# Two down projections by seven streamed products, with the sums of their operands made in gate and up

## The chip, the cores and the metric

The kernel runs on one core of a Trainium2 chip. The metric is the device time of one execution in microseconds (us); less is better. A tile has 128 partitions. Engines: PE (matrix products, into eight banks of PSUM of 128 x 512 f32), PEld (its loading of the stationary operand), DVE, ACT, POOL (elementwise work), SP (issues nearly all DMAs, in order).

## The reference

One decoder layer on x of 1024 tokens x 1024, in float32. Its two feed-forward blocks (FFN1, FFN2) are alike; the mixer between them is not touched by the change.

```python
def swiglu(x, w_gate, w_up, w_down):
    return (jax.nn.silu(x @ w_gate) * (x @ w_up)) @ w_down

x = x + 0.5 * swiglu(rmsnorm(x, ffn1_norm), ffn1_w_gate, ffn1_w_up, ffn1_w_down)
x = x + hybrid_mixer(rmsnorm(x, mix_norm), ...)
x = x + 0.5 * swiglu(rmsnorm(x, ffn2_norm), ffn2_w_gate, ffn2_w_up, ffn2_w_down)
return rmsnorm(x, final_norm)
```

w_gate and w_up are 1024 x 2816, w_down is 2816 x 1024: 22 blocks of 128 hidden features, taken in 11 pairs.

## The kernel before

**Precision.** Every operand of a large product is split in two float32r parts: a high part H (ACT casts it) and a low part L = operand - H (DVE subtracts). A product of blocks is three matmuls per 128 features: H with H, H with L, L with H. `load_w2` loads 128 x 1024 values into a `wraw` (or `xs`) buffer, casts at L204 and subtracts at L205. Loaded weights land in a pool of pairs (wH, wL). FFN1 has four raw buffers and five pairs (`wp` two and three, `wp1` two and two); FFN2's gate and up stage has four raw buffers and four pairs, its down stage four and six.

**Gate and up.** `hidden_tiles` goes over the 11 pairs, for each the gate half and then the up half. Tokens and features are both cut in two, and the four blocks of a half's result come from seven products of sums of blocks instead of eight plain ones. `seven_weights` loads two blocks of 128 weight columns and lets POOL make four sums into a tile wS (L346), of which there is one buffer; casts and subtractions follow (L354, L355). `seven_products` runs the seven products (12 matmuls of 128 x 512 each, L365) in the order 1, 2, 6, 5, 7, 4, 3; ACT copies a bank out (`ev`, L393) and DVE adds a second one to it (L397), giving four tiles `sg` or `su`. The first product of the first two pairs (EARLY = 2) is made before the rest, so these have five products left. ACT applies silu to the gate tiles. Then POOL multiplies su by sg in place (`gate_up`, L423), and SP writes the result to a DRAM buffer `hd[j]` of pair j.

**Down.** `down` runs plain products over chunks of 6, 6, 6 and 4 blocks. For each chunk, the hidden blocks come back from `hd` and the weights from w_down, both through `load_w2`; for each column half and each of eight token tiles, a bank collects all matmuls of the chunk (L537) and DVE adds half of it to x (L539). The x tiles are loaded in the first chunk, one ahead of each token tile (L552). The last chunk goes token tile by token tile, both halves, and calls `done(t)`, which in FFN1 writes x, normalises it and turns it for the mixer, and in FFN2 normalises it and writes the output. In FFN1 `done` also loads the mixer's first two weights (`first`).

**Order.** All instructions are put in order at compile time, engine by engine, by a scheduler that walks a model of the machine and takes the ready instruction of best priority (program order); each engine and each queue then runs its own list strictly in order, and waits on semaphores. A buffer of a tile tag with n buffers is given out again when all users of the earlier tile are done.

Of the kernel before, what the change touches and what calls it, by code (L numbers as in the profile page):

```python
# [9 lines left out]
F32 = mybir.dt.float32  # L10
# [6 lines left out]
P = 128  # L17
# [46 lines left out]
class Weights:  # L64
# [25 lines left out]
def psum(C, tag):  # L90
    return C.pp.tile([P, 512], F32, name=tag, tag=tag, bufs=BANKS[tag])
# [329 lines left out]
def gate_up(C, out, sg, hd, i, a, eng=None):  # L421

    (eng or C.nc.gpsimd).tensor_tensor(out=out, in0=out, in1=sg, op=ALU.mult)  # L423
    C.nc.sync.dma_start(hd[:, i, a * 512:a * 512 + 512], out)


EARLY = 2
# [54 lines left out]
    return banks  # L482


def hidden_tiles(C, XB, wg, wu, hd, banks, whole):

    nc = C.nc

    def tiles(tag, bufs):
        return [[C.fp.tile([P, 512], F32, name=tag, tag=tag, bufs=bufs) for _ in range(2)] for _ in range(2)]  # L490

    for j in range(DFF // P // 2):
        rest = ((1, 1), (1, 0), (0, 1)) if j < EARLY else ((0, 0), (1, 1), (1, 0), (0, 1))

        def half(w, tag, bufs):
            early = banks.pop(0) if j < EARLY else None
            out = tiles(tag, bufs) if whole else None
            W = seven_weights(C, w, j * 256, early is not None)
            out = out or tiles(tag, bufs)
            first = j == 0 and w is wg and not whole  # L500
            seven_products(C, W, XB, out, early, PIECES if first else WHOLE, "tC" if first else "tA")
            return out

        g = half(wg, "sg", 5)
# [7 lines left out]
def down(C, tc, x, src, wd, hd, chunks, last, done, side):  # L512

    nc = C.nc

    def hidden(f0, n, a):
        tiles = []
        for j in range(f0 // 2, (f0 + n) // 2):
            to = [C.fp.tile([P, SLOT], F32R, name=t, tag=t, bufs=8 if not C.last else 4) for t in ("hidH", "hidL")]
            H, L = load_w2(C, hd[j][:, :, a * 512:a * 512 + 512], 2, 512, to)  # L520
            tiles += [(H[:, i], L[:, i]) for i in range(2)]
        return tiles

    def wtiles(f0, n, nh):
        W = []
        for k2 in range(0, n, 2):
            r = (f0 + k2) * P
            H, L = load_w2(C, wd[r:r + 256, nh * 512:nh * 512 + 512].rearrange("(k p) n -> p k n", p=P), 2, 512)
            W += [(H[:, 0], L[:, 0]), (H[:, 1], L[:, 1])]
        return W  # L530

    def one(t, nh, hid, W):
        ps = psum(C, "tC" if nh else "mm")
        m = slice(t % 4 * P, t % 4 * P + P)
        seq = [(hid[t // 4][k][i], W[k][w]) for k in range(len(W)) for i, w in ((0, 0), (0, 1), (1, 0))]
        for i, (h, w) in enumerate(seq):
            nc.tensor.matmul(ps, h[:, m], w, start=i == 0, stop=i == len(seq) - 1)  # L537
        xs = x[t][:, nh * 512:nh * 512 + 512]
        nc.vector.scalar_tensor_tensor(xs, ps, 0.5, xs, op0=ALU.mult, op1=ALU.add)  # L539

    f0 = 0
    C.last = False
    with tc.tile_pool(name="hid", bufs=1, side=side, reuse_waits="tile") as C.fp:
        for n in chunks:
            hid = []
            for nh in (0, 1):
                W = wtiles(f0, n, nh)
                for t in range(NT):
                    if nh == 0 and t % 4 == 0:
                        hid.append(hidden(f0, n, t // 4))  # L550
                    if f0 == nh == 0:
                        nc.sync.dma_start(x[t], src[t * P:t * P + P])  # L552
                    one(t, nh, hid, W)
            f0 += n
    C.last = True
    with tc.tile_pool(name="hidl", bufs=1, side=side, reuse_waits="tile") as C.fp:
        last()
        Ws = [wtiles(f0, 4, 0), wtiles(f0, 4, 1)]
        hid = [hidden(f0, 4, a) for a in (0, 1)]
        for t in range(NT):  # L560
            for nh in (0, 1):
                one(t, nh, hid, Ws[nh])
            done(t)

# [935 lines left out]
def ffn2(C, tc, I, out, hs):  # L1500

    nc = C.nc
    wg, wu = I["ffn2_w_gate"], I["ffn2_w_up"]
    C.XB = {}
    for i, names in enumerate((("B11", "B21"), ("T2", "T1"))):
        for q, n in enumerate(names):
            C.XB[n] = [b[i][:, q * 4:q * 4 + 4, :] for b in (C.hH, C.hL)]
    with ExitStack() as st:
        x2p = st.enter_context(tc.tile_pool(name="x2", bufs=1, side="right"))

        x2 = dict((t, x2p.tile([P, D], F32, name=f"x2{t}")) for t in (0, 4, 1, 5, 2, 6, 3, 7))
        late, W2 = merge_out(C, tc, I, x2)
        with tc.tile_pool(name="xb2", bufs=1, reuse_waits="tile") as xb:
            for n in ("T3", "B22", "T4"):
                C.XB[n] = [xb.tile([P, 4, 512], F32R, name=n + h) for h in "HL"]
            with tc.tile_pool(name="lo", bufs=1) as lo:
                banks = early_products(C, I, late, W2, lo)
            st.close()
            with tc.tile_pool(name="f2", bufs=1, reuse_waits="tile") as C.fp:
                C.wp.add(C.tp, 2, 0, "xs")  # L1520
                hidden_tiles(C, C.XB, wg, wu, C.hd, banks, True)
    hs.close()
    with tc.tile_pool(name="x3", bufs=1, reuse_waits="tile") as xp:
        C.wp.add(xp, 0, 2)
        x = [xp.tile([P, D], F32, name=f"x{t}") for t in range(NT)]

        def done(t):
            y = xp.tile([P, D], F32, name="y", tag="xg", bufs=3)
            nc.gpsimd.tensor_tensor(out=y, in0=x[t], in1=C.gF, op=ALU.mult)  # L1529
            r = rstd(C, x[t], xp)  # L1530
            nc.scalar.activation(y[:, :512], y[:, :512], AF.Copy, scale=r)  # L1531
            nc.sync.dma_start(out[t * P:t * P + P, :512], y[:, :512])
            nc.vector.tensor_scalar(y[:, 512:], y[:, 512:], r, None, op0=ALU.mult)  # L1533
            nc.sync.dma_start(out[t * P:t * P + P, 512:], y[:, 512:])

        def last():
            C.gF = load_gain(C, I["final_norm"])

        down(C, tc, x, C.x2d, I["ffn2_w_down"], C.hd, (6, 6, 6), last, done, "right")


def layer(tc, I, out):
# [4 lines left out]
    with ExitStack() as st, ExitStack() as hs:  # L1547
# [17 lines left out]
        C.hd = [C.dp.tile([P, 2, T], F32, name=f"hd{j}") for j in range(DFF // P // 2)]  # L1565
        C.hH, C.hL = [None, None], [None, None]

        def open_h(a):
# [12 lines left out]
def ffn1(C, tc, I, open_h):  # L1581

    nc = C.nc
    with ExitStack() as st:
        C.wp.add(st.enter_context(tc.tile_pool(name="wp1", bufs=1)), 2, 2)
        C.tp = st.enter_context(tc.tile_pool(name="tp1", bufs=1))
        consts(C, I)
        with tc.tile_pool(name="xb", bufs=1) as xb:
            XB = {n: [xb.tile([P, 4, 512], F32R, name=n + h) for h in "HL"] for n in XBLOCKS if n != "T4"}
            wg, wu = I["ffn1_w_gate"], I["ffn1_w_up"]  # L1590
            with tc.tile_pool(name="s1", bufs=1) as sp:
                banks = early_tiles(C, tc, XB, I, wg, wu, C.hd, sp)
            with tc.tile_pool(name="f1", bufs=1, reuse_waits="tile") as C.fp:
                hidden_tiles(C, XB, wg, wu, C.hd, banks, False)
# [4 lines left out]
        with tc.tile_pool(name="x1", bufs=1, reuse_waits="tile") as xp:  # L1599
            x = []  # L1600
            for t in range(NT):
                x.append(xp.tile([P, D], F32, name=f"x{t}"))
# [12 lines left out]
                if t > 1:  # L1615
                    late.pop(0)()

            down(C, tc, x, I["x"], I["ffn1_w_down"], C.hd, (6, 6, 6), lambda: open_h(1), done1, "left")

            C.begun = {}  # L1620
            for c0, (H, L), at in ((C_QA, W[0], None), (C_KA, W[1], {5: late[1]})):
# [30 lines left out]
```

## Time and profile before

| | |
|---|---|
| Median of three runs | 2651.56 us (2649.98, 2651.56, 2662.56) |
| Profiled execution, own time | 2658.93 us |
| its span, first to last instruction | 2657.2 us |
| mean granted TensorE clock | 0.99 |
| FFN1's down matmuls (L537) | from 470.1 to 724.4 us |
| FFN2's down matmuls (L537) | from 2397.2 to 2643 us |

In the profile, "PE L537 MATMUL mm<-wH,hidH 128*128 128x512 f32 x1" is a matmul of line 537 into a bank named mm, with stationary 128 x 128 and moving 128 x 512; the first number is its start, the second its length, as far as matmuls are recorded singly. The end of a matmul is modelled, so its pace is read from starts. "[1.98 <-PE tC L365]" is the idle time of the engine just before an instruction, and what ended it. Rows of groups give busy us, the mean in ns, then idle time before and its releasers. SPq rows are DMAs at the time SP issues them; a length there that covers several DMAs includes SP's waiting between them.

### The profile page before, as it was taken

What the parts mean: (1) busy time and instruction counts of PE and PEld (TensorE: products, weight loads), DVE (VectorE), ACT (ScalarE), POOL (GpSimd) and SP (SyncE); (2) the same over time, 40 slices, a digit from 0 to 9 for tenths busy, and PEclk for the clock granted to TensorE, in tenths of its full rate; (3) what the DMA queues carried; (4) which work ended last, traced back from release to release, by engine and by line L of the source; (5) the groups of instructions that cost most, each with busy time, mean ns of one, the idle gap of its engine ahead of it and who ended that gap; (6) DMA issues with size and microseconds to landing.
All of it is one profiled execution on the core that took longest, in us unless ns stands there. A gap on an engine that the chain in (4) does not pass through costs nothing. (4 is left out here: it accounts for less than half of the span.)

```text
span 2657.2 us, 34573 instructions
## 1 busy us (share of the span) xinstructions
PE 2574.7 (97%) x13007; PEld 2140.1 (81%) x13007; DVE 1459.2 (55%) x3276; ACT 1017.2 (38%) x1706; POOL 469.6 (18%) x378
## 2 busy tenths in 40 slices
PE   6999999999999999999999999999999999999997
PEld 5888888788788888887887888877877888887886
DVE  6444444432744447868877877445764444444326
ACT  5333333211434338445444543343433333332113
POOL 5534452000200000000000000000004445430002
PEclk9999999999999999999999999999999999999999
DMA  5322223522331232223312122366533223226211
GB/s 152 91 87 88 83 73 98 202 95 64 113 95 52 75 78 58 60 73 94 83 54 63 55 62 76 122 217 227 183 99 115 76 84 88 84 80 222 99 56 72
DMA packets 298807, 262.10 MB, mean 99 GB/s; under 512 B 39856, under 2 KB 232592, under 8 KB 298640
## 3 DMA queue, kind: packets, MB, share of 16 engines
q1 hardware_dynamic: 298640, 259.90, 32.0%
q8 instruction: 102, 1.67, 0.3%
q14 instruction: 65, 0.53, 0.1%
HBM read 195.26 MB, written 58.29 MB: 95 GB/s over the span
## 5 line engine op out<-in xcount | busy, mean ns | idle before, releaser
L229 PE MATMUL mm<-hH,wH 128*128 128x512 f32 x1072 | 438.4, 409 | 0.0
L229 PE MATMUL mm<-hH,wL 128*128 128x512 f32 x1072 | 419.6, 391 | 0.1
L229 PE MATMUL mm<-hL,wH 128*128 128x512 f32 x1072 | 418.4, 390 | 0.0
L204 ACT CAST wH<-wraw 128x1024 fp32r<-128x1024 f32 (+1 forms) x138 | 143.8, 1046 | 293.6 <-PE mm L537 124.3
L205 DVE TENSOR_TENSOR wL<-wraw,wH 128x1024 fp32r<-128x1024 f32 (+1 forms) x138 | 169.5, 1230 | 127.0 <-ACT wH L204 122.2
L229 PEld LDWEIGHTS mm<-hH,wL 128*128 128x128 f32 x1072 | 201.4, 188 | 45.5 <-DVE wL L205 0.5
L229 PEld LDWEIGHTS mm<-hH,wH 128*128 128x128 f32 x1072 | 202.2, 189 | 40.4 <-issue 3.6
L229 PEld LDWEIGHTS mm<-hL,wH 128*128 128x128 f32 x1072 | 202.4, 189 | 36.0
L355 DVE TENSOR_TENSOR wL<-wS,wH 128x1024 fp32r<-128x1024 f32 x88 | 126.8, 1442 | 161.7 <-ACT wH L354 160.9
L346 POOL TENSOR_TENSOR wS<-wraw 128x512 f32<-128x512 f32 x66 | 84.1, 1296 | 564.0 <-PE tA L296 323.6
L423 POOL TENSOR_TENSOR su<-su,sg 128x512 f32<-128x512 f32 x84 | 133.2, 1596 | 185.6 <-DVE su L397 161.5
L354 ACT CAST wH<-wS 128x1024 fp32r<-128x1024 f32 x88 | 92.5, 1053 | 152.0 <-PE tC L365 110.3
L393 ACT COPY ev<-mm 128x512 f32<-128x512 f32 (+1 forms) x118 | 68.4, 580 | 199.8 <-PE mm L365 199.8
L537 PE MATMUL mm<-wH,hidH 128*128 128x512 f32 x352 | 138.2, 393 | 2.8 <-DVE x L539 2.0
L537 PE MATMUL mm<-wH,hidL 128*128 128x512 f32 x352 | 137.7, 391 | 2.6 <-DVE hidL L205 2.6
L537 PE MATMUL mm<-wL,hidH 128*128 128x512 f32 x352 | 137.5, 390 | 1.3 <-DVE wL L205 1.3
L537 PE MATMUL tC<-wH,hidH 128*128 128x512 f32 x352 | 137.2, 390 | 1.5 <-ACT wH L204 1.5
L537 PE MATMUL tC<-wL,hidH 128*128 128x512 f32 x352 | 137.8, 392 | 0.5 <-DVE wL L205 0.5
L537 PE MATMUL tC<-wH,hidL 128*128 128x512 f32 x352 | 137.7, 391 | 0.0
L922 POOL MEMSET xp<- 128x3 f32 x24 | 2.4, 100 | 584.4 <-DVE ka L728 244.6
L539 DVE SCALAR_TENSOR_TENSOR x<-mm,x 128x512 f32<-128x512 f32 x64 | 43.9, 688 | 105.6 <-PE mm L537 104.5
L539 DVE SCALAR_TENSOR_TENSOR x<-tC,x 128x512 f32<-128x512 f32 x64 | 44.0, 688 | 88.2 <-PE tC L537 88.2
(432 smaller groups left out, 5997.4 us busy)
## 6 DMA issues: line engine op xcount, KB each, us to landing
wraw<-in_w_in_dram SPq DMA_DIRECT2D x64, 512.0 KB, 4.0
wraw<-in_ffn_w_gate_dram SPq DMA_DIRECT2D x48, 512.0 KB, 4.6
hd<-su SPq DMA_DIRECT2D x84, 256.0 KB, 3.2
wraw<-in_ffn_w_down_dram SPq DMA_DIRECT2D x33, 512.0 KB, 4.6
wraw<-hd SPq DMA_DIRECT2D x33, 512.0 KB, 4.6
wraw<-in_ffn_w_up_dram SPq DMA_DIRECT2D x26, 512.0 KB, 5.0
xs<-in_ffn_w_up_dram SPq DMA_DIRECT2D x22, 512.0 KB, 3.9
wraw<-in_w_branch_b_dram SPq DMA_DIRECT2D x16, 512.0 KB, 4.3
```

The lines of the kernel that those rows point to most:

```text
L204: nc.scalar.copy(H[:, :width], raw[:, :width])
L205: (nc.gpsimd if C.pool_split else nc.vector).tensor_tensor(out=L[:, :width], in0=raw[:, :width], in1=H[:, :width].bitcast(F32), op=ALU.sub ...
L229: ins = nc.tensor.matmul(ps, w[:, k, :], x[:, k, :], start=k == 0 and i == 0, stop=k == kt - 1 and i == 2)
L346: nc.gpsimd.tensor_tensor(out=out, in0=p, in1=q, op=op)
L354: nc.scalar.copy(H[:, :n], srcs)
L355: eng.tensor_tensor(out=L[:, :n], in0=srcs, in1=H[:, :n].bitcast(F32), op=ALU.subtract)
L393: nc.scalar.copy(v[:, s], ps[:, s])
L423: (eng or C.nc.gpsimd).tensor_tensor(out=out, in0=out, in1=sg, op=ALU.mult)
L537: nc.tensor.matmul(ps, h[:, m], w, start=i == 0, stop=i == len(seq) - 1)
L539: nc.vector.scalar_tensor_tensor(xs, ps, 0.5, xs, op0=ALU.mult, op1=ALU.add)
L922: nc.gpsimd.memset(xp[:, 0:3], 0.0)
```

## The change

1. In `hidden_tiles`, from the third pair on (j >= EARLY), the result is no longer written to `hd`. `hidden_blocks` makes four sums of the pair's four blocks on POOL, over the gate tiles and one up tile, and writes seven blocks (A11, A12, A22, S1 to S4) to DRAM, in chunks of two pairs (nine pairs: four chunks of two and one of one).
2. In the up half of the next pair, behind its weight sums, `down_blocks` loads two blocks of rows of w_down, makes four sums of their halves on POOL (one of them into an up tile of the earlier pair) and writes them to DRAM (T1 to T4). The last pair's come after the loop.
3. `down` runs the nine pairs as seven products, in the order of `DOWN`. A product goes chunk by chunk: a load of its hidden operand, a load of its weight operand, and for four token tiles six matmuls per tile into four banks that stay open over the product. Two sets of four banks alternate, and some products add to what their set already holds. After each product DVE adds half of four banks to x. The x tiles are loaded behind the fourth and fifth slot of the first product and in the third.
4. Pairs 0 and 1 stay plain and come last, token tile by token tile, with `done(t)` as before.
5. Pools: the hidden tiles have four buffers instead of eight and are laid out ahead of x; FFN1's `wp1` has one pair instead of two (four in all); FFN2's down stage gets two raw buffers more (six in all, six pairs); the gain for the last norm is loaded ahead of the down stage, into the buffer that `down_blocks` uses; tiles for results of FFN2's gate and up are taken behind the weights from the second pair on.

```diff
 def gate_up(C, out, sg, hd, i, a, eng=None):
     (eng or C.nc.gpsimd).tensor_tensor(out=out, in0=out, in1=sg, op=ALU.mult)
-    C.nc.sync.dma_start(hd[:, i, a * 512:a * 512 + 512], out)
+    if hd is not None:
+        C.nc.sync.dma_start(hd[:, i, a * 512:a * 512 + 512], out)
...
+def hidden_blocks(C, u, g, n):
+    (a11, a21), (a12, a22) = u
+    s1, s2, s3, s4 = g[1][1], g[0][0], a21, g[1][0]
+    for out, p, q, op in ((s1, a21, a22, ALU.add), (s3, a11, a21, ALU.subtract), (s2, s1, a11, ALU.subtract), (s4, a12, s2, ALU.subtract)):
+        C.nc.gpsimd.tensor_tensor(out=out, in0=p, in1=q, op=op)
+    c, i = slot(n)
+    for name, v in (("A11", a11), ("A12", a12), ("A22", a22), ("S1", s1), ("S3", s3), ("S2", s2), ("S4", s4)):
+        C.nc.sync.dma_start(C.ab[name][c][:, i, :], v)
+
+def down_blocks(C, wd, n, t3):
+    nc = C.nc
+    X, Y = [pool.tile([P, SLOT], F32, name=tag, tag=tag, bufs=1) for pool, tag in ((C.tp, "gB"), (C.fp, "wY"))]
+    for i, r in enumerate((X, Y)):
+        nc.sync.dma_start(r, wd[(2 * n + i) * P:(2 * n + i + 1) * P])
+    lo, hi = slice(0, 512), slice(512, 1024)
+    for out, p, q in ((t3, Y[:, hi], X[:, hi]), (X[:, hi], X[:, hi], X[:, lo]), (Y[:, hi], Y[:, hi], X[:, hi]), (Y[:, lo], Y[:, lo], Y[:, hi])):
+        nc.gpsimd.tensor_tensor(out=out, in0=p, in1=q, op=ALU.subtract)
+    c, i = slot(n)
+    for name, v in (("T3", t3), ("T1", X[:, hi]), ("T2", Y[:, hi]), ("T4", Y[:, lo])):
+        nc.sync.dma_start(C.tb[name][c][:, i, :], v)
...
         def half(w, tag, bufs):
             early = banks.pop(0) if j < EARLY else None
-            out = tiles(tag, bufs) if whole else None
+            out = tiles(tag, bufs) if whole and j == 0 else None
             W = seven_weights(C, w, j * 256, early is not None)
+            if w is wu and due:
+                down_blocks(C, wd, *due.pop())
             out = out or tiles(tag, bufs)
...
         for i, a in rest:
-            gate_up(C, u[i][a], g[i][a], hd[j], i, a)
+            gate_up(C, u[i][a], g[i][a], hd[j] if j < EARLY else None, i, a)
+        if j >= EARLY:
+            hidden_blocks(C, u, g, j)
+            due.append((j, u[0][0]))
+    down_blocks(C, wd, *due.pop())
+
+DOWN = (("A11", "B11", 0, True, (0, 0)), ("A12", "B21", 1, True, (0, 0)), ("S2", "T2", 0, False, (0, 1)), ("S1", "T1", 1, True, (1, 1)),
+        ("S3", "T3", 0, False, (1, 1)), ("S4", "B22", 1, False, (0, 1)), ("A22", "T4", 0, False, (1, 0)))
+
+def down(C, x, src, wd, hd, done):
...
+    def hidden(v, n):
+        return load_w2(C, v, n, 512, [C.fp.tile([P, SLOT], F32R, name=t, tag=t, bufs=4) for t in ("hidH", "hidL")])
...
+    def mms(ps, m, hid, W, n, first, stop, more=False):
+        seq = [(hid[i][:, k], W[w][:, k]) for k in range(n) for i, w in ((0, 0), (0, 1), (1, 0))]
+        for i, (h, w) in enumerate(seq):
+            nc.tensor.matmul(ps, h[:, m], w, start=first and i == 0, stop=stop and i == len(seq) - 1, skip_group_check=more)
+
+    banks = [[psum(C, tag) for tag in tags for _ in range(2)] for tags in (("mm", "tM"), ("tA", "tC"))]
+    for a, b, z, begin, (half, nh) in DOWN:
+        for c, v in enumerate(C.ab[a]):
+            n = v.shape[1]
+            A, B = hidden(v, n), weights(b, c, n)
+            for t in range(4):
+                mms(banks[z][t], slice(t * P, t * P + P), A, B, n, begin and c == 0, c == len(C.ab[a]) - 1, not begin)
+            for t in {("B11", 3): (0, 1), ("B11", 4): (2, 3)}.get((b, c), (4 + c,) if b == "T2" and c < 4 else ()):
+                nc.sync.dma_start(x[t], src[t * P:t * P + P])
+        for t in range(4):
+            add(half * 4 + t, nh, banks[z][t])
+    Ws = [[weights_plain(C, wd, c, nh) for c in range(EARLY)] for nh in (0, 1)]
+    hid = [[hidden(hd[c][:, :, q * 512:q * 512 + 512], 2) for c in range(EARLY)] for q in (0, 1)]
+    for t in range(NT):
+        for nh in (0, 1):
+            ps = psum(C, "mm" if nh else "tC")
+            for c in range(EARLY):
+                mms(ps, slice(t % 4 * P, t % 4 * P + P), hid[t // 4][c], Ws[nh][c], 2, c == 0, c == EARLY - 1)
+            add(t, nh, ps)
+        done(t)
...
 (ffn2)
-    with tc.tile_pool(name="x3", bufs=1, reuse_waits="tile") as xp:
-        C.wp.add(xp, 0, 2)
+    with tc.tile_pool(name="hid", bufs=1, side="right", reuse_waits="tile") as C.fp, tc.tile_pool(name="x3", bufs=1, reuse_waits="tile") as xp:
+        C.wp.add(xp, 2, 2)
...
 (ffn1)
-        C.wp.add(st.enter_context(tc.tile_pool(name="wp1", bufs=1)), 2, 2)
+        C.wp.add(st.enter_context(tc.tile_pool(name="wp1", bufs=1)), 2, 1)
```

More of the change, by code (lines that the diff above doesn't have):

```diff
@@ L482, in early_tiles, with slot, hidden_tiles @@
     return banks
-def hidden_tiles(C, XB, wg, wu, hd, banks, whole):
+def slot(n):
+    n -= EARLY
+    return n // 2, n % 2
+def hidden_blocks(C, u, g, n):
[17 more added lines that the diff above has]
+        nc.sync.dma_start(C.tb[name][c][:, i, :], v)
+def hidden_tiles(C, XB, wg, wu, wd, hd, banks, whole):
     nc = C.nc
@@ L490, in tiles @@
         return [[C.fp.tile([P, 512], F32, name=tag, tag=tag, bufs=bufs) for _ in range(2)] for _ in range(2)]
+    due = []
     for j in range(DFF // P // 2):
@@ L508, in hidden_tiles @@
         for i, a in rest:
-            gate_up(C, u[i][a], g[i][a], hd[j], i, a)
-def down(C, tc, x, src, wd, hd, chunks, last, done, side):
-    nc = C.nc
[L516 to L537, printed above, removed]
+            gate_up(C, u[i][a], g[i][a], hd[j] if j < EARLY else None, i, a)
@@ new lines, in hidden_tiles, with weights, add @@
+        if j >= EARLY:
[5 more added lines that the diff above has]
+def down(C, x, src, wd, hd, done):
+    nc = C.nc
+    def hidden(v, n):
+        return load_w2(C, v, n, 512, [C.fp.tile([P, SLOT], F32R, name=t, tag=t, bufs=4) for t in ("hidH", "hidL")])
+    def weights(name, c, n):
+        if name in C.tb:
+            v = C.tb[name][c]
+        else:
+            i, q = int(name[1]) - 1, int(name[2]) - 1
+            j = EARLY + 2 * c
+            v = wd.rearrange("(j i p) n -> i p j n", i=2, p=P)[i][:, j:j + n, q * 512:q * 512 + 512]
+        return load_w2(C, v, n, 512)
+    def add(t, nh, ps):
@@ L538, in one @@
         xs = x[t][:, nh * 512:nh * 512 + 512]
         nc.vector.scalar_tensor_tensor(xs, ps, 0.5, xs, op0=ALU.mult, op1=ALU.add)
[L541 to L563, printed above, removed]
+    def mms(ps, m, hid, W, n, first, stop, more=False):
+        seq = [(hid[i][:, k], W[w][:, k]) for k in range(n) for i, w in ((0, 0), (0, 1), (1, 0))]
+        for i, (h, w) in enumerate(seq):
+            nc.tensor.matmul(ps, h[:, m], w, start=first and i == 0, stop=stop and i == len(seq) - 1, skip_group_check=more)
@@ new lines, in down, with weights_plain @@
+    Ws = [[weights_plain(C, wd, c, nh) for c in range(EARLY)] for nh in (0, 1)]
[7 more added lines that the diff above has]
+        done(t)
+def weights_plain(C, wd, c, nh):
+    return load_w2(C, wd[c * 256:c * 256 + 256, nh * 512:nh * 512 + 512].rearrange("(k p) n -> p k n", p=P), 2, 512)
@@ L1520, in ffn2 @@
                 C.wp.add(C.tp, 2, 0, "xs")
-                hidden_tiles(C, C.XB, wg, wu, C.hd, banks, True)
+                hidden_tiles(C, C.XB, wg, wu, I["ffn2_w_down"], C.hd, banks, True)
     hs.close()
-    with tc.tile_pool(name="x3", bufs=1, reuse_waits="tile") as xp:
-        C.wp.add(xp, 0, 2)
+    with tc.tile_pool(name="hid", bufs=1, side="right", reuse_waits="tile") as C.fp, tc.tile_pool(name="x3", bufs=1, reuse_waits="tile") as xp:
+        C.wp.add(xp, 2, 2)
         x = [xp.tile([P, D], F32, name=f"x{t}") for t in range(NT)]
@@ L1534, in done @@
             nc.sync.dma_start(out[t * P:t * P + P, 512:], y[:, 512:])
-        def last():
-            C.gF = load_gain(C, I["final_norm"])
-        down(C, tc, x, C.x2d, I["ffn2_w_down"], C.hd, (6, 6, 6), last, done, "right")
+        C.gF = load_gain(C, I["final_norm"])
+        down(C, x, C.x2d, I["ffn2_w_down"], C.hd, done)
 def layer(tc, I, out):
@@ L1564, in layer @@
         C.ud = [C.dp.tile([32, 1024], F32, name=f"ud{f}") for f in range(2)]
-        C.hd = [C.dp.tile([P, 2, T], F32, name=f"hd{j}") for j in range(DFF // P // 2)]
+        C.hd = [C.dp.tile([P, 2, T], F32, name=f"hd{j}") for j in range(EARLY)]
+        sizes = [min(2, DFF // P // 2 - j) for j in range(EARLY, DFF // P // 2, 2)]
+        C.ab = {b: [C.dp.tile([P, n, 512], F32, name=f"{b}_{c}") for c, n in enumerate(sizes)] for b, *_ in DOWN}
+        C.tb = {b: [C.dp.tile([P, n, 512], F32, name=f"{b}_{c}") for c, n in enumerate(sizes)] for b in ("T1", "T2", "T3", "T4")}
         C.hH, C.hL = [None, None], [None, None]
@@ L1593, in ffn1 @@
             with tc.tile_pool(name="f1", bufs=1, reuse_waits="tile") as C.fp:
-                hidden_tiles(C, XB, wg, wu, C.hd, banks, False)
+                hidden_tiles(C, XB, wg, wu, I["ffn1_w_down"], C.hd, banks, False)
             C.xt4.__exit__(None, None, None)
@@ L1598, in ffn1 @@
         gm = load_gain(C, I["mix_norm"])
-        with tc.tile_pool(name="x1", bufs=1, reuse_waits="tile") as xp:
+        with tc.tile_pool(name="hid", bufs=1, reuse_waits="tile") as C.fp, tc.tile_pool(name="x1", bufs=1, reuse_waits="tile") as xp:
             x = []
@@ L1616, in done1 @@
                     late.pop(0)()
-            down(C, tc, x, I["x"], I["ffn1_w_down"], C.hd, (6, 6, 6), lambda: open_h(1), done1, "left")
+            open_h(1)
+            down(C, x, I["x"], I["ffn1_w_down"], C.hd, done1)
             C.begun = {}
```

## The prediction

> **What bounds the kernel now.** I read the page first (engines, then costliest groups), then busy time by stretches of the span, then TensorE's own waits, and last the order of time inside one pair of feature blocks and at the start of a down projection.
>
> ```profile
> span 2657.2 us, 34573 instructions
> PE 2574.7 (97%) x13007; PEld 2140.1 (81%) x13007; DVE 1459.2 (55%) x3276; ACT 1017.2 (38%) x1706; POOL 469.6 (18%) x378
> ```
>
> TensorE is busy nearly all the time, but the ends of matmuls are modelled, so I look at stretches and at starts. Columns below: stretch and length; busy time (and count) of PE, PEld, DVE, ACT, POOL; granted clock, DMA share, GB/s.
>
> ```profile
> 2183.00:2221.00 38.00, 38.00 (x169) 31.49 (x168) 16.66 (x16) 13.41 (x19) 17.52 (x12) 1.00 0.29 84
> 470.00:530.00 60.00, 55.95 (x244) 45.34 (x244) 28.06 (x29) 11.59 (x11) 2.15 (x1) 1.00 0.62 211
> 530.00:590.00 60.00, 60.00 (x267) 49.69 (x266) 23.23 (x26) 12.44 (x12) 0.00 (x0) 1.00 0.27 88
> 670.00:690.00 20.00, 18.14 (x78) 14.06 (x76) 15.87 (x25) 8.34 (x10) 4.77 (x2) 1.00 0.59 178
> 2396.00:2456.00 60.00, 56.58 (x240) 45.48 (x239) 27.58 (x29) 16.50 (x16) 3.23 (x2) 0.97 0.64 221
> 2600.00:2620.00 20.00, 19.52 (x87) 15.81 (x86) 14.67 (x37) 6.93 (x11) 5.79 (x3) 1.00 0.19 67
> ```
>
> The first row is one pair in FFN2's gate and up stage: no gap on TensorE, and DVE, ACT and POOL under half. The third is the middle of FFN1's down projection: no gap again. The other four hold all the gaps of the two down stages that matter: 4.05 and 3.42 us at their starts, 1.86 and 0.48 us at the turn to the last four blocks, 9.8 us together. So both stages in question are set by the number of matmuls times their pace. The pace, from two starts that are 24 matmuls and two changes of bank apart:
>
> ```profile
> 2611.79 0.39 PE L537 MATMUL mm<-wH,hidH 128*128 128x512 f32 x1
> 2617.23 0.39 PE L537 MATMUL mm<-wH,hidH 128*128 128x512 f32 x1
> ```
>
> 5.44 us / 24 = 0.2267 us. The count (one row of six alike, for both down projections):
>
> ```profile
> L537 PE MATMUL mm<-wH,hidH x352: 387/389/774, 470.3 to 2640.4; 128*128 128x512 f32 x176
> ```
>
> 6 x 352 = 2112, that is 1056 in each: 22 blocks x 8 token tiles x 2 column halves x 3 terms.
>
> **The change part by part.**
>
> *Fewer matmuls.* Pairs 0 and 1 stay plain: 4 blocks x 8 x 2 x 3 = 192. The other nine pairs are seven products of 9 blocks (half of 18) x 4 token tiles x 3 terms = 108 matmuls: 756. So 948 instead of 1056 each, 216 fewer in all. Stationary 128x128, moving 128x512, as before, so at the pace above: 216 x 0.2267 = **-49.0 us**. The banks change every 6 matmuls; the two changes inside the 5.44 us cost nothing visible.
>
> *Sums of hidden blocks and down weights, in gate and up.* Each of nine pairs per FFN gains eight POOL operations on 128x512 (hidden_blocks 4, down_blocks 4). POOL now, over FFN1's steady pairs:
>
> ```profile
> L423 POOL TENSOR_TENSOR su<-su,sg 128x512 f32<-128x512 f32 x37 | 58.7, 1606 | 76.0 <-DVE su L397 76.0
> L346 POOL TENSOR_TENSOR wS<-wraw 128x512 f32<-128x512 f32 x36 | 45.7, 1291 | 126.4 <-DVE wL L355 126.4
> L346 POOL TENSOR_TENSOR wS<-wraw,wS 128x512 f32<-128x512 f32 x18 | 28.6, 1590 | 1.4
> ```
>
> Each is 1.29 us alone, 1.6 us on average where it meets other work. Eight more are 10.3 to 12.8 us; a pair goes from 17.5 to about 28 to 30 us of its 168 x 0.2267 = 38.1 us. It fits; the question is what is queued behind. In order of time for one FFN2 pair:
>
> ```profile
> 2246.13 1.29 POOL L423 TENSOR_TENSOR su<-su,sg 128x512 f32<-128x512 f32 x1 [1.10 <-issue]
> 2248.57 2.54 POOL L346 TENSOR_TENSOR wS<-xs 128x512 f32<-128x512 f32 x2 [1.16 <-DVE wL L355]
> 2252.45 2.17 POOL L346 TENSOR_TENSOR wS<-xs,wS 128x512 f32<-128x512 f32 x1
> 2256.04 1.05 ACT L354 CAST wH<-wS 128x1024 fp32r<-128x1024 f32 x1 [1.98 <-PE tC L365]
> 2266.59 2.54 POOL L346 TENSOR_TENSOR wS<-wraw 128x512 f32<-128x512 f32 x2 [11.97 <-DVE wL L355]
> 2238.08 1.23 DVE L355 TENSOR_TENSOR wL<-wS,wH 128x1024 fp32r<-128x1024 f32 x1 [3.33 <-ACT wH L354]
> 2246.21 2.29 DVE L355 TENSOR_TENSOR wL<-wS,wH 128x1024 fp32r<-128x1024 f32 x1 [0.22 <-ACT wH L354]
> 2231.76 0.69 DVE L397 TENSOR_TENSOR su<-ev,tM 128x512 f32<-128x512 f32 x1 [3.33 <-PE tM L365]
> 2269.59 0.39 PE L365 MATMUL mm<-hH,wH 128*128 128x512 f32 x1
> ```
>
> The last multiply of the pair ends at 2247.4. If the four block sums go next they end at 2252.6 and push the weight sums from 2254.6 to about 2258.7, so the cast that now starts at 2256.0 moves by some 2.7 us. The product that reads these weights is the third of the next half (mm, last row): it starts at 2269.6. After the cast, to 2259.8, and its subtraction that leaves about 8 us; the cover is the weights' lead of half a pair. The four down-weight sums then run from 2258.7 to 2264, just ahead of the weight sums at 2266.6. I take **0**; bounds 0 to +18 us (1 us on each of 18 pairs). Tiles: sums overwrite gate and up tiles, which are free again only once written out. The one that goes into the first up tile is made by about 2260, landing takes 3.2 us (row below), and DVE's first up result of the next pair comes at 2231.8 + 38.1 = 2269.9.
>
> The two wL rows show the price of company: the same subtraction takes 1.23 us alone and 2.29 us when it starts with a POOL operation. With eight more POOL operations a pair, DVE loses at most 8 x 1.06 = 8.5 us, from 16.7 to 25 of 38.1 us: hidden.
>
> [...]
>
> *Queue of SP.* A pair issues 17 DMAs instead of 8 (4 weight loads, 2 down-weight loads, 7 block writes, 4 weight-sum writes): 6 x 0.52 + 11 x 0.26 = 6.0 MB in 38.1 us, 158 GB/s instead of 83. SP waits in order, so weight loads can now stand behind writes that wait for POOL:
>
> ```profile
> 306.70 14.99 SPq L424 DMA_DIRECT2D hd<-su  x3
> ```
>
> It already stands 15 us for three such writes, in a stretch without gaps. Taken at 0, covered by the same lead.
>
> *The stream.* A slot is one product x one chunk of two blocks: 24 matmuls, 5.44 us, and needs two 512 KB loads, two casts and two subtractions. There are 31.5 such slots per FFN; today a chunk of six blocks has 12 loads for 288 matmuls (65 us).
>
> ```profile
> L204 ACT CAST wH<-wraw 128x1024 fp32r<-128x1024 f32 (+1 forms) x138 | 143.8, 1046 | 293.6 <-PE mm L537 124.3
> L205 DVE TENSOR_TENSOR wL<-wraw,wH 128x1024 fp32r<-128x1024 f32 (+1 forms) x138 | 169.5, 1230 | 127.0 <-ACT wH L204 122.2
> L539 DVE SCALAR_TENSOR_TENSOR x<-mm,x 128x512 f32<-128x512 f32 x64 | 43.9, 688 | 105.6 <-PE mm L537 104.5
> ```
>
> ACT 2 x 1.05 = 2.1 us, DVE 2 x 1.23 + 28 adds x 0.69 / 35 = 3.0 us, of 5.44. DMA: 1.05 MB / 5.44 us = 193 GB/s. What limits is how soon a raw buffer comes round; FFN1 has four, FFN2 six. One round in today's start of FFN2's down stage, from issue to the next issue into it:
>
> ```profile
> 2392.76 0.52 SPq L203 DMA_DIRECT2D xs<-hd  x1
> 2398.34 1.05 ACT L204 CAST hidH<-xs 128x1024 fp32r<-128x1024 f32 x1 [1.43 <-DMA xs<-hd]
> 2399.42 1.23 DVE L205 TENSOR_TENSOR hidL<-xs,hidH 128x1024 fp32r<-128x1024 f32 x1 [1.25 <-ACT hidH L204]
> 2400.68 0.53 SPq L203 DMA_DIRECT2D xs<-hd  x1
> ```
>
> 7.92 us with others in flight: four buffers give a load each 1.98 us, where 2.72 are needed. Four slots of split tiles ahead (four hidden, four weight pairs) hold 16 to 22 us of work. So the stream keeps TensorE fed.
>
> *Its start and the x loads.* DMA at FFN2's start today (2376 to 2460 us) as 40 slices of 2.1 us in GB/s, and medians of us to landing:
>
> ```profile
> GB/s 0 186 63 0 8 129 239 7 228 262 303 321 214 293 207 268 415 423 410 414 403 389 317 15 0 0 218 31 0 181 84 271 256 207 236 21 36 278 305 130
> x<-x2d SPq DMA_DIRECT2D x8, 512.0 KB, 8.8
> wraw<-hd SPq DMA_DIRECT2D x33, 512.0 KB, 4.6
> hd<-su SPq DMA_DIRECT2D x84, 256.0 KB, 3.2
> ```
>
> The eight x tiles come at up to 423 GB/s and hold back the rest. The change puts them behind the fourth slot and later, and an add that waits for x no longer holds a bank that the next product needs (four banks alternate over 24 us). Against that stand a need for loads twice as high and POOL's last eight sums beside the first slots. I take the 9.8 us of gaps as unchanged: **0**, between -9.8 and +10.
>
> *FFN1's pool of weight pairs goes from five to four.*
>
> ```profile
> 680.10 1.05 ACT L204 CAST wH<-wraw 128x1024 fp32r<-128x1024 f32 x1 [0.83 <-DMA wraw<-in_w_in_dram]
> 721.23 1.82 ACT L204 CAST wH<-wraw 128x1024 fp32r<-128x1024 f32 x2
> ```
>
> FFN2 has four already, and its row above shows no gap. At the end the four last weights hold all pairs, so the mixer's first weight, cast 40 us ahead today (first row; the down stage's last tile begins near the second), is cast once the first of them is free, some 18 matmuls (4 us) before it is needed; a cast and a subtraction are 2.3 us. **+1 us**, bounds 0 and +2.5. The opening of FFN1 I take as 0, at most +2.3.
>
> **Sum.** -49.0 + 1.0 = -48.0 us. The profiled execution took 2658.9 us (1.7 around its span): 2610.9. The three runs' median is 2651.56, 7.4 below it; from that, **2603.6 us**.
>
> **Rivals.** *The stream is bound by its loads* (faster, but less). If the x loads' landing of 8.8 instead of 4.6 us held for all loads of FFN1's stream, a round would be 7.9 + 4.2 = 12.1 us, a slot of two loads from four buffers 6.05 us, +0.61 x 31.5 = +19 us: 2623 us. For it: the row at 2396 with gaps and 221 GB/s. Against: those gaps fall in a crush that lasts some 15 us.
>
> *The queue of SP or the chain block sums, weight sums, writes makes each half late* (no change). 36 halves, each 1.36 us late, eat the 49 us: about 2651. The weights would have to come some 8 us later than worked out above before the first loss.
>
> *POOL becomes the bound of gate and up* (slower). A pair has 20 POOL operations; today's mean is 17.52 / 12 = 1.46 us. At the 2.17 us of the slowest one above, all 20 take 43.4 us, 5.3 over the 38.1: 18 x 5.3 = +95, so about 2699 us. It decides from (38.1 + 49.0/18) / 20 = 2.04 us per operation. Against: most stand at 1.29.
>
> *The matmuls fall but their pace worsens* by the bank changes: the 0.2267 us holds across two changes, so I give it nothing.
>
> **How the numbers follow.** Forecast 0.73 (own range 2592 to 2614, by the start's bounds), load-bound 0.12, no change 0.08, slower 0.07. Range 2590 to 2630: the forecast and the load-bound case, less some of their edges. A change under 0.5% (13 us) can't be told from none here, as the three runs alone spread over 12.6 us. Faster 0.85, same 0.08, slower 0.07.
>
> **What the changed profile would show.** 1896 matmuls in the down stages, PE busy near 2526 us; a pair in gate and up still 38 of 38 us, with POOL at 28 to 30; gaps of down starts within a few us of today's; no repeated wait of PE on a cast, hidL or wL inside the stream. Total POOL 655 to 700 us. About 342 MB moved in place of 262. Wrong if a pair's period exceeds 38.1 us, or a slot's exceeds 5.44 us again and again.

## The result, and the profile after

The changed kernel takes 2625.43 us (median of four runs, 2621.67 to 2626.83) where the kernel before takes 2650.99 us in the same comparison (2649.98 to 2662.56): 25.6 us less, ratio 0.9892, 95% interval 0.9862 to 0.9921 (21 to 37 us). Two later comparisons, with more runs of the kernel before (9 and 11), gave 2623.46 against 2657.28 us (0.9873, 0.9859 to 0.9886) and 2621.82 against 2655.61 us (0.9880, 0.9865 to 0.9896): 33.8 us less, twice. The profiled spans differ by as much, 2657.2 - 2622.5 = 34.7 us. So the gain is some 34 us where 48 were forecast, and the missing 14 us are what had to be found.

The page of the changed kernel (its span, its first engines row and its DMA row):

```profile
span 2622.5 us, 35003 instructions
PE 2522.4 (96%) x12791; PEld 2097.7 (80%) x12791; DVE 1515.5 (58%) x3304; ACT 1072.7 (41%) x1774; POOL 694.9 (26%) x522
DMA packets 325789, 342.37 MB, mean 131 GB/s; under 512 B 43536, under 2 KB 236272, under 8 KB 325616
```

216 matmuls fewer (12791 instead of 13007), PE busy 52 us less, POOL 225 us more. Busy time by stretches (same columns as in the prediction): a pair of FFN2's gate and up, then 60 us from the start and two from the middle of FFN1's stream, and the start of FFN2's.

```profile
2207.00:2245.00 38.00, 38.00 (x169) 31.49 (x168) 17.39 (x17) 13.38 (x19) 29.75 (x21) 1.00 0.47 158
469.80:529.80 60.00, 49.07 (x206) 39.80 (x205) 30.55 (x27) 17.37 (x20) 15.00 (x9) 0.91 0.76 266
529.80:589.80 60.00, 60.00 (x266) 49.69 (x265) 34.40 (x38) 23.34 (x26) 0.00 (x0) 1.00 0.62 209
589.80:649.80 60.00, 60.00 (x267) 49.69 (x266) 29.26 (x31) 21.49 (x23) 0.00 (x0) 1.00 0.57 187
2379.60:2439.60 60.00, 47.60 (x200) 38.43 (x199) 26.21 (x27) 18.82 (x20) 11.97 (x9) 0.89 0.80 291
```

The pair and the middle of the stream have no gap. The new waits are in the two starts, 10.93 and 12.40 us of idle time, where before 4.05 and 3.42 stood. One row of TensorE's waits holds nearly all of it (us in total, times, the longest):

```profile
PE mm L581 <- ACT wH L204: 22.7, 2, 12.4
```

TensorE waits for the cast of a weight, twice. The timeline shows why (a choice of its rows): SP, POOL, ACT and PE at FFN1's start, then SP, ACT and PE at FFN2's. S and T are the DRAM buffers of the block sums and of the down-weight sums.

```profile
473.09 2.15 POOL L497 TENSOR_TENSOR sg<-su 128x512 f32<-128x512 f32 x1
475.27 0.33 SPq L500 DMA_DIRECT2D S<-sg  x1
479.74 1.69 SPq L500 DMA_DIRECT2D S<-sg  x2
482.34 0.32 SPq L515 DMA_DIRECT2D T<-su  x1
485.07 1.26 POOL L512 TENSOR_TENSOR wY<-wY 128x512 f32<-128x512 f32 x1
485.02 1.66 SPq L515 DMA_DIRECT2D T<-wY  x2
486.77 0.39 SPq L203 DMA_DIRECT2D wraw<-in_ffn_w_down_dram  x1
490.96 1.04 ACT L204 CAST wH<-wraw 128x1024 fp32r<-128x1024 f32 x1 [21.00 <-DMA wraw<-in_ffn_w_down_dram]
492.06 1.22 PE L581 MATMUL mm<-wH,hidH 128*128 128x512 f32 x2 [10.32 <-ACT wH L204]
...
2392.21 1.66 SPq L515 DMA_DIRECT2D T<-wY  x2
2394.44 0.40 SPq L203 DMA_DIRECT2D wraw<-A  x1
2400.13 1.99 ACT L204 CAST hidH<-wraw 128x1024 fp32r<-128x1024 f32 x2 [20.96 <-DMA wraw<-A]
2403.12 1.22 PE L581 MATMUL mm<-wH,hidH 128*128 128x512 f32 x2 [12.40 <-ACT wH L204]
```

Read it upwards from PE's wait. The weight's load was issued at 486.77, just behind the last write of a down-weight sum, and that write waited for the last of POOL's eight sums of the last pair (473.09 to 486.33). The stream's load waits for none of these sums; it merely stands behind them on SP's list, and ACT is idle 21 us for it. FFN2 repeats it, with the load of the last norm's gain (issued at 2393.96) between the last write and the stream's load.

### The profile page after: what moved, and what is told of

Read it like the earlier page. It is cut to its first block, busy times and chain, and to the rows that moved or that the text cites. A ratio compares the mean times of both kernels' runs of the same rounds, so it can differ in the third digit from the quotient of the medians.

```text
span 2622.5 us, 35003 instructions
## 1 busy us (share of the span) xinstructions
PE 2522.4 (96%) x12791; PEld 2097.7 (80%) x12791; DVE 1515.5 (58%) x3304; ACT 1072.7 (41%) x1774; POOL 694.9 (26%) x522
## 2 busy tenths in 40 slices
DMA packets 325789, 342.37 MB, mean 131 GB/s; under 512 B 43536, under 2 KB 236272, under 8 KB 325616
## 5 line engine op out<-in xcount | busy, mean ns | idle before, releaser
L205 DVE TENSOR_TENSOR wL<-wraw,wH 128x1024 fp32r<-128x1024 f32 (+2 forms) x171 | 205.0, 1200 | 141.6 <-ACT wH L204 138.0
L204 ACT CAST wH<-wraw 128x1024 fp32r<-128x1024 f32 (+2 forms) x171 | 173.4, 1018 | 190.2 <-PE mm L229 71.1
L204 ACT CAST hidH<-wraw 128x1024 fp32r<-128x1024 f32 (+1 forms) x64 | 62.4, 979 | 152.9 <-PE tM L581 56.3
L205 DVE TENSOR_TENSOR hidL<-wraw,hidH 128x1024 fp32r<-128x1024 f32 (+1 forms) x64 | 77.2, 1211 | 79.2 <-ACT hidH L204 79.0
L581 PE MATMUL mm<-wH,hidH 128*128 128x512 f32 x208 | 82.3, 398 | 22.7 <-ACT wH L204 22.7
L354 ACT CAST wH<-wraw 128x512 fp32r<-128x512 f32 (+1 forms) x60 | 49.0, 817 | 93.5 <-PE tM L365 48.6
L581 PE MATMUL mm<-wH,hidL 128*128 128x512 f32 x208 | 82.1, 395 | 0.6 <-DVE hidL L205 0.6
L581 PE MATMUL mm<-wL,hidH 128*128 128x512 f32 x208 | 82.5, 396 | 0.0
L355 DVE TENSOR_TENSOR wL<-wraw,wH 128x512 fp32r<-128x512 f32 (+1 forms) x60 | 75.6, 1260 | 4.6 <-ACT wH L354 3.7
L979 DVE SCALAR_TENSOR_TENSOR ka<-xp,cw,ka 128x512 f32<-128x512 f32 x96 | 72.2, 754 | 5.2 <-ACT ka L977 4.4
```

What stands on the lines that cost most here:

```text
L204: nc.scalar.copy(H[:, :width], raw[:, :width])
L205: (nc.gpsimd if C.pool_split else nc.vector).tensor_tensor(out=L[:, :width], in0=raw[:, :width], in1=H[:, :width].bitcast(F32), op=ALU.sub ...
L354: nc.scalar.copy(H[:, :n], srcs)
L355: eng.tensor_tensor(out=L[:, :n], in0=srcs, in1=H[:, :n].bitcast(F32), op=ALU.subtract)
L581: nc.tensor.matmul(ps, h[:, m], w, start=first and i == 0, stop=stop and i == len(seq) - 1, skip_group_check=more)
L979: nc.vector.scalar_tensor_tensor(o, x, w, o, op0=ALU.mult, op1=ALU.add)
```

## The experiments

Theory Q: at the hand-over from gate and up to the stream, the last pair's writes, waiting on SP for POOL, hold the stream's loads. Its rivals: the raw buffers come round too slowly; the traffic of DMAs is too heavy; the place of the x loads. Line numbers behind the edits are one higher than in the changed kernel (its L581 is L582).

**The base.** The changed kernel again, beside the first three edits and beside the next group; the last group has the fastest version as its base.

> The changed kernel once more, as the measure for the three others on the same chip. All theories: 2622 to 2627 us, and in its profile TensorE stands still once in each FFN about two to four slots into the stream, 10.3 us in FFN1 and 12.4 us in FFN2, 22.7 us together.

> The changed kernel once more, as the base for the other three of this batch: gaps on PE at the stream's start near 10.8 us (FFN1) and 12.4 us (FFN2), time 34 us under the kernel before, ratio near 0.987.

Measured: 2623.46 and 2621.82 us, as above; the two waits come to 23.3 and 23.0 us.

**More work on POOL in the last pair.** T3 of the last pair is computed five times instead of once (the further four repeat the first); SP's order is unchanged.

```diff
-        nc.gpsimd.tensor_tensor(out=out, in0=p, in1=q, op=ALU.subtract)
+        for _ in range(5 if n == DFF // P // 2 - 1 and out is t3 else 1):
+            nc.gpsimd.tensor_tensor(out=out, in0=p, in1=q, op=ALU.subtract)
```

> The changed kernel with T3 of the last pair computed five times over instead of once: four more POOL operations of 1.28 us, 5.1 us, ahead of the four T writes, with the same order on SP. Queue theory: each gap grows by 5.1 us, to about 15.4 and 17.5 us, and the time by 10 us, to about 2635 us. Buffer theory: the four subtractions of the hidden tiles are over before the added operations start in FFN1 (478.6 against 481.0 us), so less than 2 us more. Traffic theory: no change.

Measured: 2636.08 us (2632.52 to 2641.16), 12.6 us more than the base of its batch; ratio to the kernel before 0.9920 (0.9906 to 0.9933). TensorE's wait in this kernel:

```profile
PE mm L582 <- ACT wH L204: 33.4, 2, 17.7
```

33.4 instead of 23.3 us: each start waits 5 us longer, about the time of four POOL operations (4 x 1.3), as the queue theory expected. Of the 12.6 us the waits make 10.1; the rest isn't settled. Nothing was added to DMA traffic or buffers, so these two rivals don't explain it; the sums are on the path of the load.

**The last pair's writes on POOL's own queue.** POOL issues the S and T writes of the last pair itself.

```diff
 # hidden_blocks
-        C.nc.sync.dma_start(C.ab[name][c][:, i, :], v)
+        q = C.nc.gpsimd if n == DFF // P // 2 - 1 and name[0] == "S" else C.nc.sync
+        q.dma_start(C.ab[name][c][:, i, :], v)
 # down_blocks
-        nc.sync.dma_start(C.tb[name][c][:, i, :], v)
+        (nc.gpsimd if n == DFF // P // 2 - 1 else nc.sync).dma_start(C.tb[name][c][:, i, :], v)
```

> The last pair's S and T writes (eight in each FFN) are issued by POOL behind its own sums instead of by SP; all sums and all bytes stay. Queue theory (SP stands behind writes that wait for POOL, and the stream's loads are queued behind them): FFN1's gap of 10.3 us falls under 3 us. In FFN2 the load of the last norm's gain still stands on SP ahead of the stream's loads, and it waits for the write of T1, so FFN2's gap stays at 9 to 13 us: in all 7 to 11 us less than the changed kernel, about 2616 us. Buffer theory (raw buffers come free late, since the subtractions beside POOL's sums take up to twice as long; the loads could not have started sooner): both gaps stay within 2 us of 10.3 and 12.4, the time within 3 us of the changed kernel. Traffic theory (the x tiles and writes crowd the DMA engines): as the buffer theory.

Measured: 2622.70 us (2619.85 to 2626.79), ratio 0.9871 (0.9857 to 0.9884): no better than its base. The old gap of FFN1 is gone, but the timeline has a new one:

```profile
470.81 2.60 SPq L203 DMA_DIRECT2D wraw<-in_ffn_w_down_dram  x2
480.11 0.71 SPq L203 DMA_DIRECT2D wraw<-A  x1
487.24 0.56 POOL L516 DMA_DIRECT2D T<-gB  x1
491.28 0.33 SPq L242 DMA_DIRECT2D gB<-in_mix_norm_dram  x1
491.71 0.38 SPq L203 DMA_DIRECT2D wraw<-in_ffn_w_down_dram  x1
498.16 0.80 PE L582 MATMUL tA<-wH,hidH 128*128 128x512 f32 x1 [3.91 <-ACT wH L204]
...
2391.13 0.33 SPq L242 DMA_DIRECT2D gB<-in_final_norm_dram  x1
```

By the first row two weight loads go out by 473.4, where the changed kernel had the next one at 486.77: their raw buffers were free, and it was the place on SP's list that had held them. SP stands from 480.8 to 491.28, now for the load of the next norm's gain: its buffer gB is the one that `down_blocks` works in, and it is free only when T1's write (issued by POOL at 487.24) has landed. In FFN2 the same gain load is issued at 2391.13 and the wait there grew from 12.4 to 16.1 us: counted from the stream's first matmul (at 2373.8 here, at 2379.7 in the changed kernel) the gain load is issued 17.3 us later, where it was 14.3 us. It now waits for T1's landing, and POOL issues its writes between the sums. One DMA waiting at the head of the queue was replaced by another, which had been hidden behind the first. The expectation was right on the place in FFN1 and wrong on FFN2 and on the total.

**The gain loads too.** In addition both gain loads go on POOL's queue.

```diff
-def load_gain(C, g):
+def load_gain(C, g, q=None):
...
-    C.nc.sync.dma_start(gB, bass.AP(...))
+    (q or C.nc.sync).dma_start(gB, bass.AP(...))
...
-        C.gF = load_gain(C, I["final_norm"])
+        C.gF = load_gain(C, I["final_norm"], nc.gpsimd)
...
-        gm = load_gain(C, I["mix_norm"])
+        gm = load_gain(C, I["mix_norm"], nc.gpsimd)
```

> As the run with the last pair's sums written from POOL's queue, and the two gain loads (mix norm, final norm) are issued by POOL too. Queue theory: both gaps fall under 3 us, 18 to 23 us less than the changed kernel, 2603 to 2607 us, which is where the prediction's sum stood. Buffer theory and traffic theory: both gaps stay, time within 3 us of the changed kernel.

> The version with the last pair's S and T writes and both gain loads on POOL's queue once more, as the base for the next one: 14 us under the changed kernel, with one gap of 8.1 us left at the start of FFN2's stream and none over 1 us in FFN1's.

Measured: 2609.46 us (2607.39 to 2614.80), ratio 0.9823 (0.9809 to 0.9836), 14.0 us under the base of its batch; again on another chip 2608.53 us, ratio 0.9829 (0.9814 to 0.9844), 13.3 under the base. That is less than the 18 to 23 us expected, since only FFN1's gap is gone. One wait of 8.1 us is left, at FFN2's start, and its releaser is another engine. The wait, and two rows of DVE from the timeline, in the second run:

```profile
PE mm L582 <- DVE wL L205: 8.1, 1, 8.1
2383.19 1.59 DVE L205 TENSOR_TENSOR wL<-xs,wH 128x512 fp32r<-128x512 f32 x1 [12.28 <-DMA S<-sg]
2384.70 3.53 DVE L205 TENSOR_TENSOR hidL<-wraw,hidH 128x1024 fp32r<-128x1024 f32 x2
```

A subtraction into a weight buffer waits 12.28 us until a block sum has been written out. FFN2's down stage takes two pairs of weight buffers from the pool that lies where the gate tiles were. DVE takes its list in order, so the hidL subtractions behind it wait too: in the first run their casts are done at 2376.57, and they start at 2384.02.

**FFN2's stream without the two pairs over the gate tiles.**

```diff
-        C.wp.add(xp, 2, 2)
+        C.wp.add(xp, 2, 0)
```

> The version with the last pair's writes and the gain loads on POOL's queue, and FFN2's stream without the two extra wH, wL pairs that lie over a gate tile of the last pair (four pairs of buffers in place of six, as FFN1 has). Theory A, the 8.1 us gap left in FFN2 is DVE standing in order behind the subtraction into such a wL, which must let an S write land first: the gap goes to under 3 us, and the time falls by 5 to 9 us against the version it is built on, to some 41 us under the changed kernel's 34 (47.8 + 5 to 9, so 53 to 57 under the kernel before). Rival B, the loads are late in FFN2 whatever DVE waits for (their raw buffers, DMA traffic): the gap stays at 6 to 9 us and the time within 2 us. Rival C, four pairs are too few for the stream: new gaps spread over the stream's 216 us, total up by 5 us or more.

> The version with the last pair's writes and the gain loads on POOL's queue and four pairs of weight buffers in FFN2's stream once more, as the base for the next one: 57 us under the kernel before, no gap over 2 us at either start of the stream.

Measured: 2597.95 us (2595.07 to 2600.45), ratio 0.9788 (0.9772 to 0.9804), and on another chip 2598.69 us (2595.55 to 2606.33), ratio 0.9798 (0.9776 to 0.9821). That is 10.6 us under the version it is built on, more than the 5 to 9 expected, and 23.9 under the changed kernel of the same batch; the fastest version here, 57.7 us under the kernel before. Stretches with the starts of both streams (second run):

```profile
462.00:522.00 60.00, 59.39 (x263) 48.82 (x262) 41.89 (x35) 25.04 (x27) 23.17 (x20) 1.00 0.87 313
2366.00:2426.00 60.00, 58.70 (x260) 48.27 (x259) 37.31 (x34) 22.62 (x25) 17.60 (x18) 1.00 0.89 333
```

0.6 and 1.3 us of gaps are left. Four pairs are enough for the stream: at its matmuls (L582) TensorE's waits list one of 1.3 and one of 0.6 us and no others, and from 2420 to 2480 us TensorE is busy 60.00 of 60 us. Of the 10.6 us, the wait gives 8.1 - 1.3 = 6.8 and the slow matmuls behind it (0.42 to 0.43 us apart from 2390.02 to 2393.86; see below) some 2; where the last 2 us come from isn't settled.

**The buffers alone.** The same edit on the changed kernel, without moving any write.

> The changed kernel with FFN2's two extra pairs of weight buffers over a gate tile left out and nothing moved between queues. Theory A, in the changed kernel SP's queue is the later of the two waits and the buffer shows only once that is gone: the gap of 12.4 us in FFN2 stays at 11 to 13 us and the time within 2 us of the changed kernel (33 us under the kernel before). Rival B, the buffer is the cause in FFN2 by itself: that gap falls to 3 to 5 us and the time by 7 to 9 us.

Measured: 2622.26 us (2620.44 to 2625.80), ratio 0.9886 (0.9866 to 0.9906), as the changed kernel. TensorE's wait:

```profile
PE mm L581 <- ACT wH L204: 22.2, 2, 11.8
```

With SP's queue as it was, the load comes so late that the buffer doesn't show. The edit is worth 0 alone and 10.6 us behind the other two: the three waits lay one behind the other. (The comparison with the changed kernel goes through the kernel before: 33.8 us less, as there.)

**More sums in the steady pairs.** T3 of pairs 2 to 9 is computed three times, the last pair as it was.

```diff
-        nc.gpsimd.tensor_tensor(out=out, in0=p, in1=q, op=ALU.subtract)
+        for _ in range(3 if n < DFF // P // 2 - 1 and out is t3 else 1):
+            nc.gpsimd.tensor_tensor(out=out, in0=p, in1=q, op=ALU.subtract)
```

> The changed kernel with T3 of the steady pairs 2 to 9 of both FFNs computed three times in place of once (32 more POOL subtractions of 128x512 in all, of 1.2 to 2.2 us each), the last pair as it is. Theory A, the sums of the steady pairs lie beside the matmuls: POOL is busy about 2 x 1.5 to 2.2 us more per pair (33 to 34 of 38 us in place of 29.75), PE stays without gaps there, time within 3 us of the changed kernel, and the gaps at the two starts stay 10.8 and 12.4. Rival B, POOL or the writes behind its sums on SP already set the pair's pace: each further subtraction costs its own 1.2 to 2.2 us, 38 to 69 us in all.

Measured: 2630.77 us (2629.95 to 2635.91), ratio 0.9917 (0.9903 to 0.9930), 9.0 us more than its base; neither theory's number. Two steady pairs of it, one in each FFN:

```profile
214.00:252.00 38.00, 38.00 (x169) 31.49 (x168) 18.30 (x16) 13.48 (x18) 33.31 (x23) 1.00 0.49 159
2104.00:2142.00 38.00, 38.00 (x170) 31.45 (x169) 18.07 (x16) 13.40 (x19) 33.34 (x23) 1.00 0.50 160
```

POOL 33.3 of 38 us and still no gap: in steady pairs the sums are hidden, with room to spare. The loss that can be placed is in FFN1's last pair and the stream's start: from 420 to 540 us 437 matmuls are counted where the base has 474, so 37 x 0.2267 = 8.4 us. (The two profiled executions lie 15.1 us apart, more than the medians; the other 6.7 us are spread over later stages and not explained.) Pair 9's sums are made inside the last pair's up half, and there the next loads on SP are already the stream's. The timeline of that place, and the same cast in the base:

```profile
468.99 1.04 ACT L204 CAST wH<-wraw 128x1024 fp32r<-128x1024 f32 x1 [8.97 <-DMA wraw<-in_ffn_w_down_dram]
470.06 1.22 DVE L205 TENSOR_TENSOR wL<-wraw,wH 128x1024 fp32r<-128x1024 f32 x1 [10.17 <-ACT wH L204]
471.94 0.79 PE L365 MATMUL tC<-B22H,wH 128*128 128x512 f32 x1 [4.39 <-DVE su L397]
```

```profile
463.41 1.05 ACT L204 CAST wH<-wraw 128x1024 fp32r<-128x1024 f32 x1 [3.00 <-DMA wraw<-in_ffn_w_down_dram]
```

Here a weight of the stream is late, DVE waits for it in order, and the results of gate and up queue behind it on DVE, so a bank comes free late.

**The x loads in front.** The fastest version, with all eight x loads behind the stream's first slot.

```diff
-            for t in {("B11", 3): (0, 1), ("B11", 4): (2, 3)}.get((b, c), (4 + c,) if b == "T2" and c < 4 else ()):
+            for t in range(NT) if (b, c) == ("B11", 0) else ():
```

> That version with all eight x loads issued behind the stream's first slot, in place of four behind the fourth and fifth slots and four behind the slots of the third product: four to six further loads of 0.5 MB then stand on SP's queue ahead of the weight loads that the stream's first products wait for. Theory A, the queue and the DMA traffic at the start decide: 2 to 3 MB more at the 200 to 270 GB/s of those stretches are 8 to 15 us, of which some 5 us are covered by loads already landed; a gap of 3 to 10 us returns at each start and the time rises by 6 to 20 us. Rival B, the place of the x loads is of no weight (they are hidden wherever they stand): gaps stay under 2 us and the time within 2 us.

Measured: 2620.19 us (2615.67 to 2621.99), ratio 0.9878 (0.9857 to 0.9899), 21.5 us more than its base. The timeline of SP and PE:

```profile
468.59 4.29 SPq L593 DMA_DIRECT2D x<-in_x_dram  x8
485.66 1.22 PE L582 MATMUL mm<-wH,hidH 128*128 128x512 f32 x2 [5.14 <-ACT wH L204]
...
2371.70 4.34 SPq L593 DMA_DIRECT2D x<-x2d  x8
2394.99 1.22 PE L582 MATMUL mm<-wH,hidH 128*128 128x512 f32 x2 [13.31 <-ACT wH L204]
```

The gaps return, larger than expected in FFN2, and the time lies just above the 6 to 20 us of theory A. Here none of the sums' writes stands on SP, and the eight loads take only 4.3 us to issue. But 4 MB go ahead of the stream's next operands; FFN1's next weight load, issued at 473.63, is cast only at 484.56. So the place of the x loads is worth some 21 us once the queue is clear, and traffic at the start is a cost as well, though not the one that the changed kernel paid.

## Why the prediction was right or wrong

- **Matmuls, -49.0: right.** 12791 matmuls, gaps apart the pace is the old one; 60 us hold 266 or 267, as before.
- **Sums in gate and up, 0: right.** A pair is 38 of 38 us with POOL at 29.75, inside the 28 to 30 foreseen, and stays so at 33.3. POOL's total of 694.9 and the 342.37 MB are also as foreseen. Of the two rivals there, neither took place.
- **The stream is fed, 0: right.** No gap in its middle; the load-bound rival falls, although the changed kernel's time lies on the number that it gave (2623). The number alone would have shown the wrong cause.
- **Queue of SP, 0: the step that failed.** It was read from a stretch of steady pairs, where SP stood 15 us without a gap, and "covered by the same lead" was carried over to the last pair. There the eight sums are not made beside a further pair, and what stands behind their writes is the operand that the next product needs: 22.7 us of waiting, in two places.
- **The stream's start, 0 with bounds of ±10: mis-sized, by the same step.** It named POOL's last eight sums, but as work beside the first slots, and not as what SP waits for. By counts of matmuls in 60 us: after, 206 and 200 of 266 and 267, that is 127 x 0.2267 = 28.8 us lost; before, by the rows at 470 and 2396, 244 and 240 of 267, 50 x 0.2267 = 11.3, and 2.3 at the turns, which are gone now. The term is +15.2 us, outside its bound. -49.0 + 15.2 = -33.8, the difference measured twice. That it fits to the decimal is chance: from FFN1's last down matmul to FFN2's first product of gate and up (L365), where the forecast has only its +1 us, three executions of the changed kernel take 1236.1 to 1239.1 us, and the profiled one before 1232.0.
- **FFN1's weight pairs, +1:** not seen apart from the rest.
- **The base.** The forecast was set on 2651.56, the median of three runs, and said that the profiled one lay 7.4 us higher. The comparisons with 9 to 11 runs have 2655.6 to 2657.3, so some 5 us of the distance of 21.8 between 2603.6 and 2625.43 belong to the base.
- **The range: luck.** The time worked out from the start's bounds was 2592 to 2614, and 2625.43 lies outside it. It lies within 2590 to 2630 because that range was widened for the load-bound case, which did not take place. The direction and the matmuls' share were foreseen; what took 15 us of it was not.

With the starts cleared, the fastest version gains 57.7 and 57.3 us: the 49.0 of the matmuls, and 8 to 9 of the 13.6 that the kernel before lost at its own starts and turns.

## What to carry to other kernels

A queue that stands long without a gap (SP 14.99 us in the steady pairs here) shows that it has a lead there, not that it has one everywhere: where stages meet, list what is queued behind each waiting DMA, and ask whether that wait is one it needs. Move such writes to the queue of the engine that makes the data, and when one wait is taken away, look for the next in the list (a load into a reused buffer, a subtraction into a reused tile), because a gain may show only when all are gone. A bound for a start is worked out as the time of the last producer's whole chain plus one landing (in FFN1 the sums end at 486.33, the weight's load is issued at 486.77, and its cast starts at 490.96), not from the gaps of the old start.

## What the runs showed of the hardware

Behind its two long gaps the changed kernel's matmuls started at a slower pace. The timeline behind the gap of 10.32 us:

```profile
494.35 0.63 PE L581 MATMUL mm<-wH,hidL 128*128 128x512 f32 x1
494.78 0.63 PE L581 MATMUL mm<-wH,hidH 128*128 128x512 f32 x1
...
496.94 0.39 PE L581 MATMUL mm<-wL,hidH 128*128 128x512 f32 x1
497.16 0.39 PE L581 MATMUL mm<-wH,hidL 128*128 128x512 f32 x1
```

For about 4 us they start 0.43 us apart, then 0.22 to 0.24; behind the gap of 12.40 us too they start 0.42 to 0.43 us apart between 2405.35 and 2407.91, then 0.23. The granted clock of the stretch is 0.91, and 0.89 in FFN2. Some 4 us at 0.43 in place of 0.2267 us from start to start make, as an estimate, some 2 us that such a gap cost beyond its length, and that the waits of TensorE don't list. Before, with single gaps of 2 us at the most, the stretch at 470 had 1.00; but the one at 2396, with gaps of 1.5 us at the most, had 0.97 (starts 0.42 to 0.43 us apart between 2412.44 and 2415.00), so the length of a single gap doesn't settle it.

DVE and POOL both took longer where they ran side by side at the start of FFN1's stream. Four hidL subtractions there, before (1.43 us each) and after (1.98 us each):

```profile
471.15 5.72 DVE L205 TENSOR_TENSOR hidL<-wraw,hidH 128x1024 fp32r<-128x1024 f32 x4
```

```profile
470.65 7.91 DVE L205 TENSOR_TENSOR hidL<-wraw,hidH 128x1024 fp32r<-128x1024 f32 x4
```

POOL's operations beside them took 2.15 to 2.27 us (one is its row at 473.09 above), and 1.26 to 1.29 us from 479.79 on, when DVE was done; so FFN1's eight sums took 13.2 us (473.09 to 486.33) and not 8 x 1.29 = 10.3. This is not what makes the gap: in FFN2 seven of the eight took 1.26 to 1.29 us, and the gap there is the longer one. And the write that POOL issued itself at 487.24 took 0.56 us of its time (the row in the run with the writes on POOL's queue); its next subtraction starts at 487.82.
